# Rotary embedding over eight batches: row 0 of batch 0 is stored behind rows 1 to 15, and the first five batches are loaded without a store between

## The chip, the cores and the metric

The kernel runs on one core of one Trainium2 chip. The metric is the device time of one execution in microseconds (us). The kernel before took 316.6 us in the median of three runs (316.54 to 318.12).

## The reference

`x` is 8 x 2048 x 16 x 64 in f32 (batch, sequence, heads, head size), `cos` and `sin` are 2048 x 32. The first and second half of each head are rotated against one another:

```python
x1 = x[..., :head_dim // 2]
x2 = x[..., head_dim // 2:]
cos = cos[None, :, None, :]
sin = sin[None, :, None, :]
out1 = x1 * cos - x2 * sin
out2 = x1 * sin + x2 * cos
return np.concatenate([out1, out2], axis=-1).astype(np.float32)
```

## The kernel before, in words

**Tiling.** Of a batch's 2048 positions, partition p of 128 holds 16 neighbouring ones. These 16 are the "rows" in what follows (index j, `J` = 16): "row 0" of a batch is the first position of every partition, 128 x 1024 values, 512 KB in f32. A whole batch is 8 MB in f32. On the chip the work is in f16: `buf` (line 47) has five places of one batch each, and batch b has place b mod 5.

**Transfers.** All big transfers are issued by POOL (GpSimd) and change the type on the way: `load` (L62, issue on L71) reads f32 and writes f16 into `buf`; `store` (L73, issue on L81) reads f16 and writes f32 to the output. A call with n = 2 moves two batches in one transfer. `in_ring` (L51) ties each of them to the one before, so that POOL issues them in the order written; it makes POOL wait for nothing. The waits come from the data: a store waits for VectorE's last operation on its rows, a load for the landing of the stores that read its place of `buf`. POOL issues in order, so whatever is written behind a waiting store waits too. All of POOL's transfers are in queue q0. SP (SyncE) has q1: at the start it issues `sin` (L40), the first two rows of batch 0 into the f32 tile `head` (L41) and `cos` (L45), at the end one store of the last two rows of batch 7 (L135).

**Arithmetic.** ScalarE turns `sin`, `cos` and `head` into f16 (L104 to L110); `head` goes into rows 0 and 1 of batch 0's place (L106), so load 0 brings only rows 2 to 15. `rotate` (L83) does three VectorE operations on a batch in place: the halves swapped and multiplied by sin into `v` (L92), the batch multiplied by cos (L98), and the sum (L100). Batch 0 is rotated in two calls, rows 0 and 1 first (`JA` = 2), then rows 2 to 15.

**Order around the change.** It is written out by hand from L102 on. Loads 0 and 1 are issued; rows 0 and 1 are rotated (L111); row 0 is stored (L112); then come loads 2+3 in one transfer and load 4 (L113, L114); rows 2 to 15 of batch 0 are rotated (L115) and its rows 1 to 15 stored (L116); rotate 1 and store 1, rotate 2 and store 2 (L117 to L120); loads 5+6 and 7 (L121, L122), which take the places of batches 0, 1 and 2; then rotate 3 and 4 and store both, 5 and 6 and store both, and rotate 7, which leaves in three parts (L130, L131, L135).

Of the kernel before, what the change touches and what calls it, by code (L numbers as in the profile page):

```python
# [1 line left out]

# [4 lines left out]


@with_exitstack  # L10
def kernel(
    ctx: ExitStack,
    tc: tile.TileContext,
    x: bass.AP,
    cos: bass.AP,
    sin: bass.AP,
    out: bass.AP,
):
    nc = tc.nc
    f16 = mybir.dt.float16  # L20
    f32 = mybir.dt.float32

    B, S, H, D = x.shape
    Dh = D // 2
    P = nc.NUM_PARTITIONS
    J = S // P
    NBUF = 5

    const_pool = ctx.enter_context(tc.tile_pool(name="rope_const", bufs=1))
    io_pool = ctx.enter_context(tc.tile_pool(name="rope_io", bufs=1))  # L30
    tmp_pool = ctx.enter_context(tc.tile_pool(name="rope_tmp", bufs=1))

    JA = 2
    head = const_pool.tile([P, JA, H, D], f32)
    x0 = x[0].rearrange("(p j) h d -> p j (h d)", j=J)
    sin_f = const_pool.tile([P, J, Dh], f32)
    cos_f = const_pool.tile([P, J, Dh], f32)
    cos_h = const_pool.tile([P, J, Dh], f16)
    sin_h = const_pool.tile([P, J, D], f16)
    nc.sync.dma_start(out=sin_f, in_=sin.rearrange("(p j) d -> p j d", j=J))  # L40
    nc.sync.dma_start(  # L41
        out=head.rearrange("p j h d -> p (j h d)"),
        in_=x0[:, 0:JA, :].rearrange("p j f -> p (j f)"),
    )
    nc.sync.dma_start(out=cos_f, in_=cos.rearrange("(p j) d -> p j d", j=J))  # L45

    buf = io_pool.tile([P, NBUF, J, H, D], f16)

    ring = []

    def in_ring(dma):  # L51
        if ring:
            tc.add_manual_dep(
                dma.ins,
                ring[-1].ins.name,
                mybir.DependencyInfo(mybir.DependencyClass.NoSync, mybir.DependencyReason.DATA),
                reason="order of the ring",
            )
        ring.append(dma)
        return dma  # L60

    def load(b, n=1):  # L62
        k = b % NBUF
        if n == 1:
            j0 = JA if b == 0 else 0
            dst = buf[:, k, j0:J, :, :].rearrange("p j h d -> p (j h d)")
            src = x[b].rearrange("(p j) h d -> p j (h d)", j=J)[:, j0:J, :].rearrange("p j f -> p (j f)")
        else:
            dst = buf[:, k : k + n, :, :, :].rearrange("p b j h d -> p b (j h d)")
            src = x[b : b + n].rearrange("b (p j) h d -> p b (j h d)", j=J)  # L70
        in_ring(nc.gpsimd.dma_start(out=dst, in_=src))  # L71

    def store(b, n=1, j0=0, j1=J):  # L73
        k = b % NBUF
        if n == 1:
            src = buf[:, k, j0:j1, :, :].rearrange("p j h d -> p (j h d)")
            dst = out[b].rearrange("(p j) h d -> p j (h d)", j=J)[:, j0:j1, :].rearrange("p j f -> p (j f)")
        else:
            src = buf[:, k : k + n, :, :, :].rearrange("p b j h d -> p b (j h d)")
            dst = out[b : b + n].rearrange("b (p j) h d -> p b (j h d)", j=J)  # L80
        return in_ring(nc.gpsimd.dma_start(out=dst, in_=src))  # L81

    def rotate(b, j0=0, j1=J):  # L83
        v = tmp_pool.tile([P, J, H, D], f16)
        n = j1 - j0
        js = slice(j0, j1)
        xt = buf[:, b % NBUF, js, :, :]
        shape = [P, n, H, 2, Dh]
        sin_b = sin_h[:, js, :].rearrange("p j (e d) -> p j e d", e=2).unsqueeze(2).to_broadcast(shape)
        cos_b = cos_h[:, js, :].unsqueeze(2).to_broadcast([P, n, 2 * H, Dh])  # L90
        xe = xt.rearrange("p j h (e d) -> p j h e d", e=2)
        nc.vector.tensor_mul(  # L92
            out=v[:, js, :, :].rearrange("p j h (e d) -> p j h e d", e=2),
            in0=xe[:, :, :, ::-1, :],
            in1=sin_b,
        )
        xw = xt.rearrange("p j h (e d) -> p j (h e) d", d=Dh)
        nc.vector.tensor_mul(out=xw, in0=xw, in1=cos_b)  # L98
        xa = xt.rearrange("p j h d -> p (j h d)")
        nc.vector.tensor_add(out=xa, in0=xa, in1=v[:, js, :, :].rearrange("p j h d -> p (j h d)"))  # L100

    load(0)  # L102
    load(1)
    nc.scalar.copy(out=sin_h[:, :, Dh:D], in_=sin_f)  # L104
    nc.scalar.mul(out=sin_h[:, :, 0:Dh], in_=sin_f, mul=-1.0)  # L105
    nc.scalar.copy(  # L106
        out=buf[:, 0, 0:JA, :, :].rearrange("p j h d -> p (j h d)"),
        in_=head.rearrange("p j h d -> p (j h d)"),
    )
    nc.scalar.copy(out=cos_h, in_=cos_f)  # L110
    rotate(0, 0, JA)  # L111
    store(0, 1, 0, 1)  # L112
    load(2, 2)  # L113
    load(4)  # L114
    rotate(0, JA, J)  # L115
    store(0, 1, 1, J)  # L116
    rotate(1)  # L117
    store(1)
    rotate(2)
    store(2)  # L120
    load(5, 2)  # L121
    load(7)  # L122
    rotate(3)
    rotate(4)
    store(3, 2)
    rotate(5)
    rotate(6)
    store(5, 2)
    rotate(7)
    gate = store(7, 1, 0, 9)  # L130
    store(7, 1, 9, J - JA)  # L131
    last = buf[:, 7 % NBUF, J - JA : J, :, :].rearrange("p j h d -> p (j h d)")
    dst = out[B - 1].rearrange("(p j) h d -> p j (h d)", j=J)[:, J - JA : J, :].rearrange("p j f -> p (j f)")
    nc.scalar.copy(out=head.rearrange("p j h d -> p (j h d)"), in_=last)  # L134
    end = nc.sync.dma_start(out=dst, in_=head.rearrange("p j h d -> p (j h d)"))  # L135
    tc.add_manual_dep(
        end.ins,
        gate.ins.name,
        mybir.DependencyInfo(mybir.DependencyClass.Sync, mybir.DependencyReason.DATA),
        reason="the last rows go out behind this part",  # L140
    )


# [1 line left out]
_INS = ['x', 'cos', 'sin']  # L145
_OUTS = [((8, 2048, 16, 64), 'float32')]


# [23 lines left out]
```

## Time and profile before

| What | Value |
|---|---|
| Median of three runs | 316.6 us |
| The profiled execution's own time | 316.6 us |
| Its span | 314.8 us |
| VectorE (DVE) busy | 209.1 us, 66%, 27 operations |
| ScalarE (ACT) busy | 6.8 us |
| POOL busy | 8.6 us |
| One VectorE operation on a whole batch | 8.69 us |
| VectorE idle before L92, mostly for a load | 51.4 us |
| POOL idle before a store (L81), for VectorE's sum | 219.4 us |
| POOL idle before a load (L71), mostly for stores to land | 49.7 us |

The span runs from the first instruction of the profile to the last. "Busy" counts the engine's own operations; an instruction that issues a transfer is over long before its data has moved. Idle time of an engine is put down to what ended it. Of an issue the profile gives the size and the time until the transfer has landed; a load's size there is that of its f16 side, a store's that of its f32 side.

### The profile page before, as it was taken

To read this page: it belongs to the slowest core of one execution; us is meant where nothing else is said; L and a number is where in the kernel's file an instruction comes from. 1 tells how busy PE (TensorE), PEld (TensorE's weight loads), DVE (VectorE), ACT (ScalarE), POOL (GpSimd) and SP (SyncE) were. 2 spreads that over 40 slices of the span, in tenths; PEclk is the share of its full clock that TensorE was granted. 3 is DMA by queue.
4 is the path that set the end of the run, shared out by engine and by line. 5 is a ranking of instruction groups with operands and counts; after the bars stand their busy time and mean duration, and the time that the engine had idled before them with its cause. 6 is when DMAs were issued, how large, how long until landed. Compare 5 with 4: busy or idle time off the path is not lost.

```text
span 314.8 us, 115 instructions
## 1 busy us (share of the span) xinstructions
DVE 209.1 (66%) x27; ACT 6.8 (2%) x6; POOL 8.6 (3%) x18
## 2 busy tenths in 40 slices
DVE  0105999999499999999950000899999999910000
ACT  3200000000000000000000000000000000020000
POOL 1002000000000000000010000000000000010000
DMA  9899999999999899999999999999999999999998
GB/s 284 187 262 200 200 266 200 200 262 204 200 200 317 382 492 407 400 400 533 400 200 208 258 200 200 229 237 333 400 491 441 400 400 525 408 400 400 433 427 339
DMA packets 3104, 101.71 MB, mean 323 GB/s; under 512 B 288, under 2 KB 288, under 8 KB 672
## 3 DMA queue, kind: packets, MB, share of 16 engines
q0 software_dynamic: 2528, 99.09, 98.1%
q1 hardware_dynamic: 576, 2.62, 2.2%
HBM read 67.63 MB, written 67.11 MB: 428 GB/s over the span
## 4 chain that ended last, share of the span: by engine, by line
DVE 66%; another core or an unknown queue 13%; DMA 8%; ACT 1%; issue 0%; SPq 0%; DVEq 0%; ACTq 0%
DVE buf L98 22%; DVE buf L100 22%; DVE v L92 22%; DMA cos_f<-in_cos_dram 8%; ACT head L134 1%; ACT cos_h L110 0%; SPq L41 0%; SPq L40 0%; DVEq L92 0%; ACTq L134 0%
## 5 line engine op out<-in xcount | busy, mean ns | idle before, releaser
L92 DVE TENSOR_TENSOR v<-buf,sin_h 128x16384 f16<-128x16384 f16 (+2 forms) x9 | 69.7, 7744 | 51.4 <-DMA buf<-in_x_dram 41.2
L98 DVE TENSOR_TENSOR buf<-buf,cos_h 128x16384 f16<-128x16384 f16 (+2 forms) x9 | 69.7, 7744 | 15.8 <-ACT cos_h L110 15.5
L100 DVE TENSOR_TENSOR buf<-buf,v 128x16384 f16<-128x16384 f16 (+2 forms) x9 | 69.7, 7744 | 0.3
L81 POOL DMA_DIRECT2D out_dram<-buf x8 | 4.7, 586 | 219.4 <-DVE buf L100 219.4
L134 ACT CAST head<-buf 128x2048 f32<-128x2048 f16 x1 | 1.9, 1898 | 249.9 <-DVE buf L100 249.9
L71 POOL DMA_DIRECT2D buf<-in_x_dram x6 | 3.7, 628 | 49.7 <-DMA out_dram<-buf 48.9
L106 ACT CAST buf<-head 128x2048 f16<-128x2048 f32 x1 | 1.9, 1897 | 3.5 <-DMA head<-in_x_dram 3.5
L104 ACT ACT_TABLE_LOAD x1 | 1.3, 1283 | 0.7 <-PEq L156 0.7
L110 ACT CAST cos_h<-cos_f 128x512 f16<-128x512 f32 x1 | 0.6, 617 | 16.1 <-DMA cos_f<-in_cos_dram 16.1
L104 ACT CAST sin_h<-sin_f 128x512 f16<-128x512 f32 x1 | 0.6, 617 | 1.4 <-DMA sin_f<-in_sin_dram 1.4
L105 ACT ACTIVATE sin_h<-sin_f 128x512 f16<-128x512 f32 x1 | 0.6, 624 | 0.0
L156 POOL MEMSET const-float32-0.0<- 128x1 f32 x1 | 0.1, 100 | 0.2 <-issue 0.2
L156 POOL MEMSET const-bfloat16-1.0<- 128x1 bf16 x1 | 0.1, 103 | 0.0
L156 POOL MEMSET const-float32-1.0<- 128x1 f32 x1 | 0.1, 100 | 0.0
L156 POOL MEMSET const-uint8-127<- 128x1 uint8 x1 | 0.1, 100 | 0.0
## 6 DMA issues: line engine op xcount, KB each, us to landing
buf<-in_x_dram POOLq DMA_DIRECT2D x2, 8192.0 KB, 55.2
buf<-in_x_dram POOLq DMA_DIRECT2D x3, 4096.0 KB, 57.4
out_dram<-buf POOLq DMA_DIRECT2D x1, 7680.0 KB, 68.3
out_dram<-buf POOLq DMA_DIRECT2D x1, 4608.0 KB, 28.6
buf<-in_x_dram POOLq DMA_DIRECT2D x1, 3584.0 KB, 22.3
out_dram<-buf POOLq DMA_DIRECT2D x1, 2560.0 KB, 34.1
head<-in_x_dram SPq DMA_DIRECT2D x1, 1024.0 KB, 6.9
out_dram<-head SPq DMA_DIRECT2D x1, 1024.0 KB, 8.4
```

Of the source, the lines that this page charges most:

```text
L71: in_ring(nc.gpsimd.dma_start(out=dst, in_=src))
L81: return in_ring(nc.gpsimd.dma_start(out=dst, in_=src))
L92: nc.vector.tensor_mul(out=v[:, js, :, :].rearrange("p j h (e d) -> p j h e d", e=2), in0=xe[:, :, :, ::-1, :], in1=sin_b,)
L98: nc.vector.tensor_mul(out=xw, in0=xw, in1=cos_b)
L100: nc.vector.tensor_add(out=xa, in0=xa, in1=v[:, js, :, :].rearrange("p j h d -> p (j h d)"))
L104: nc.scalar.copy(out=sin_h[:, :, Dh:D], in_=sin_f)
L105: nc.scalar.mul(out=sin_h[:, :, 0:Dh], in_=sin_f, mul=-1.0)
L106: nc.scalar.copy(out=buf[:, 0, 0:JA, :, :].rearrange("p j h d -> p (j h d)"), in_=head.rearrange("p j h d -> p (j h d)"),)
L110: nc.scalar.copy(out=cos_h, in_=cos_f)
L134: nc.scalar.copy(out=head.rearrange("p j h d -> p (j h d)"), in_=last)
L156: nc = _bacc.Bacc("TRN2", target_bir_lowering=False, num_devices=1)
```

## The change

Row 0's store no longer stands ahead of loads 2+3 and 4, but behind the store of rows 1 to 15 and ahead of rotate 1. Loads 2+3 and 4 are issued right behind loads 0 and 1, ahead of ScalarE's first instruction in the text. The transfers themselves, their sizes and shapes stay, as do all operations of VectorE and ScalarE.

```diff
     load(0)
     load(1)
+    load(2, 2)
+    load(4)
     nc.scalar.copy(out=sin_h[:, :, Dh:D], in_=sin_f)
...
     nc.scalar.copy(out=cos_h, in_=cos_f)
     rotate(0, 0, JA)
-    store(0, 1, 0, 1)
-    load(2, 2)
-    load(4)
     rotate(0, JA, J)
     store(0, 1, 1, J)
+    store(0, 1, 0, 1)
     rotate(1)
     store(1)
```

## The prediction

> **What bounds the kernel now.** I read the page's slices and queue rows first, then the chain of waits, then the timeline of POOL (which issues all big transfers), then windows cut at the landings. The profiled execution took 316.6 us, span 314.8, so 1.8 us lie outside the span; 316.6 is also the median of the three runs.
>
> ```profile
> DMA  9899999999999899999999999999999999999998
> ...
> q0 software_dynamic: 2528, 99.09, 98.1%
> q1 hardware_dynamic: 576, 2.62, 2.2%
> HBM read 67.63 MB, written 67.11 MB: 428 GB/s over the span
> ```
>
> The 16 DMA engines are busy in every slice, and POOL's queue q0 has 98.1% of their time. 134.7 MB cross HBM. The chain of waits, in order of time, seems to say otherwise:
>
> ```profile
> 69.70 8.69 DVE buf L100
> 78.40 4.89 another core or an unknown queue
> ...
> 153.19 8.69 DVE buf L100
> 161.88 36.10 another core or an unknown queue
> ```
>
> It names VectorE for 66%, but twice breaks off at a transfer: VectorE starts again at 83.3 when the load of batches 2 and 3 has landed, and at 198.0 when that of batches 5 and 6 has. The second gap, 36.1 us, is the queue's doing. Who feeds the queue, and how early?
>
> ```profile
> 1.24 1.21 POOL L71 DMA_DIRECT2D buf<-in_x_dram  x2 [0.80 <-PEq L167]
> ...
> 29.53 0.54 POOL L81 DMA_DIRECT2D out_dram<-buf  x1 [27.08 <-DVE buf L100]
> 30.06 1.26 POOL L71 DMA_DIRECT2D buf<-in_x_dram  x2
> ...
> 52.52 0.54 POOL L81 DMA_DIRECT2D out_dram<-buf  x1 [21.19 <-DVE buf L100]
> ```
>
> POOL issues loads 0 and 1 at 1.24, then waits 27 us for VectorE's sum of the first two rows, issues row 0's store, and 0.5 us later the loads of 2, 3 and 4. These are late only for POOL. From issue to landing, the store and the first of the loads took:
>
> ```profile
> out_dram<-buf POOLq DMA_DIRECT2D x1, 512.0 KB, 15.2
> buf<-in_x_dram POOLq DMA_DIRECT2D x1, 8192.0 KB, 53.2
> ```
>
> Load 1 (issued about 1.85, landing 41.6 us later) lands at 43.5, row 0's store at 29.53 + 15.2 = 44.7, loads 2 and 3 at 30.06 + 53.2 = 83.3. So the store waits 14 us in the queue, and the loads behind it are handed over 14.6 us before the engines can begin them. The same is done for the rest: load 4 lands at 102.6, the stores of batch 0's other rows, 1 and 2 at 120.8, 140.1 and 159.4, loads 5+6 and 7 at 198.0 and 217.3, stores 3+4 and 5+6 at 256.0 and 294.6. In windows cut there (DMA share and GB/s are last; a load's GB/s count its f16 side, half of what it reads):
>
> ```profile
> 44.70:83.30 38.60, 33.59 (x4) 0.00 (x0) 1.08 (x2) 1.00 1.01 217
> 83.30:102.60 19.30, 19.15 (x3) 0.00 (x0) 0.00 (x0) 1.00 1.00 241
> 102.60:120.80 18.20, 18.13 (x3) 0.00 (x0) 0.53 (x1) 1.00 1.02 436
> 120.80:140.10 19.30, 19.23 (x3) 0.00 (x0) 0.00 (x0) 1.00 1.02 435
> ```
>
> The share is 1.0 throughout. One batch (8.39 MB of f32) takes 19.3 us in either direction, 435 GB/s: 38.6 / 2 for the loads, 19.3 for a store. The kernel is one full queue from the first packets to the last, and its time is the sum of the queue's parts.
>
> On this the Trainium skill (DMA: Bandwidth & Descriptors, "Where 436 GB/s comes from") says two things: the ports allow 435 GB/s, but for transfers between HBM and SBUF the HBM's share of about 358 GB/s binds. By the second, 134.7 MB would take 376 us, an estimate; the trace's 435 GB/s decides against it here.
>
> **The change, part by part.**
>
> *Row 0's store leaves the stretch between the loads.* The queue loses 44.7 - 43.5 = about 1.25 us there (0.524 MB at 435 GB/s would be 1.21). Loads 2+3 land at 82.0, load 4 at 101.3.
>
> *It comes back behind that of rows 1 to 15.* It needs the sum of rows 0 and 1 alone (VectorE done at 29.2), and POOL issues it right behind the other one, at about 53. The queue reaches them at 101.3: rows 1 to 15 land at 119.5 (18.2 later), row 0 at 120.8. From there on store 1 lands at 140.1 as before. What can its cost be in the new place? The trace has no small store between two big stores. In the records its 128 packets took 0.189 us each, eight per engine, 1.51 us; the landings say 1.25, since neighbours overlap. Upper end: nothing overlaps, +0.26. Lower end: it costs its bytes at full rate and a turn from load to store and back is saved, -0.05; more can't go, as its bytes remain. I take 0, by the near agreement of 1.25 with 1.21, and keep -0.05 to +0.26.
>
> *Loads 2, 3 and 4 are issued at about 2.5 to 3.7.* The row at 30.06 gives 1.26 us of POOL for both issues. Behind them on POOL is the store of rows 1 to 15, which waits for VectorE until 52.2, so this delays nobody. They wait for no buffer: five exist and these are first used here. What is queued per engine rises little: eight packets per batch make 8 + 8 + 16 + 8 = 40 at 3.7 us, against about 5 + 8 + 16 + 8 = 37 at 31.3 before. If POOL had to wait for room, it would have until 43.5 to hand over loads 2 and 3. The cost is 0 from these sides. Only the very start is not covered: a queue that starts empty (below).
>
> *VectorE.* Batch 2's first product starts at 82.0 in place of 83.3, and store 2 can be issued at 108.5 in place of 109.8. The queue wants it at 140.1: 31 us early instead of 30. Loads 5+6 wait on POOL for the landings of both stores of batch 0 and of store 1, at 140.1 as before, 19 us ahead of their turn at 159.4. Later orders keep their times: store 3+4 is issued at 162.2 and wanted at 217.3, store 5+6 at 250.7 and wanted at 256.0. That last cover, 5.3 us, is the thinnest, and both of its ends hang on the landing at 198.0, so it does not shrink. The last stores (276.9, wanted at 294.6) and SP's closing store follow.
>
> **Sum:** -1.25 + 1.25 + 0 = 0; span 314.8, time 316.6 us.
>
> **Rivals.**
>
> *The chain view is right* and the 1.25 us gained at 83.3 reaches the end: 315.3 (-0.4%). For it: the 4.89 us wait is on the chain. Against: the next one, 36.1 us, ends at a landing that the queue sets, and in a full queue row 0's bytes have only moved. Only a dry queue after 83.3 could keep the gain, and the windows show none.
>
> *Four issues in a row hold up the first load* (slower than before). Place: load 0 at the start.
>
> ```profile
> 3.00:5.00 2.00, 0.00 (x0) 1.15 (x2) 0.00 (x0) 1.00 0.98 415
> 5.00:8.00 3.00, 0.00 (x0) 0.00 (x0) 0.00 (x0) 1.00 1.53 346
> ```
>
> From 3 to 5 us the engines are at 0.98 with SP's head rows; load 0's first packet starts at 5.28 in the packet records, just as the head's last ones end (5.6), though POOL issued it at 1.24. Either it was ready and stood behind the head, or its descriptors came at 5.3 because load 1's were made first. In the second case two more issues hurt. Mild form: the 1.26 us of POOL are added, load 0 starts at 6.5, +1.26 at most, 317.9 (+0.4%); SP's cos packets would fill part. Strong form: 4.04 us for two issues (1.24 to 5.28) become 8.1 for four, load 0 starts at 9.3, some 4.0 late, of which cos (eight packets of about 0.1 us per engine) fills 0.8: +3.2, 319.8 (+1.0%). It decides from the point where the descriptors come later than 5.6, when the head is through. For it: no record shows any of load 0's packets among the head's. Against: POOL's rows show each issue as an instruction of its own, 0.6 us.
>
> By the Trainium skill (the same page, "Latency and other measured facts") POOL's path has its first byte after about 1 us, and (in "Queues, rings and completion order") an engine takes turns between its queues packet by packet. By both, load 0 would have mixed with the head from about 3 us, and the change would leave the start alone. After 7.3 us cos and load 0 do alternate in the records; before 5.28 load 0 is absent, so at least one of the two does not hold there. That is why this rival keeps a chance.
>
> *The rate changes* when 40 MB of loads run with no store between. Witness against: load batches before and after row 0's store, and 5 to 7 behind three whole stores, all take 19.3 (load 1 takes 19.9 with cos beside it). 0.5% of the time would need 2% on the 78 us of loads 1 to 4; the rows differ by 0.3%. Prices: 318.2 or 315.0.
>
> *The change does not do what it says*: POOL issues loads 2 to 4 later than 3.7 for some reason. Up to 43.5 that gives 316.6 too, so it stands with the forecast.
>
> **How the numbers follow.** A measurement here tells about 0.5% (1.6 us) from no change. Forecast (316.6, with the late issue): 0.78, same. Mild start delay (up to 317.9): 0.08, same. Strong start delay (319.8): 0.06, slower. Chain view (315.3): 0.03, same. Rate: 0.05, slower 0.03, faster 0.02. So faster 0.02, same 0.89, slower 0.09. Range: below, 316.6 - 0.05 - 0.6 for the scatter of runs (the three shown differ by up to 1.6, though two by 0.06) gives 315.9. Above, 316.6 + 0.26 + 1.26 gives 318.1. Outside lie the strong delay, the chain view and the rate, 0.14.
>
> **What would show it.** Right: loads 2+3 landing at 82.0 and VectorE's first product of batch 2 there; POOL issuing four loads by 3.8; rows 1 to 15 landing at 119.5, row 0 at 120.8, store 1 at 140.1; VectorE's wait before batch 5 ending at 198.0 and now 37.4 us long; DMA slices all 9 (or 8). Wrong: a DMA gap at 5 to 9 us and everything after it shifted alike (start rival); a landing at 198.0 that comes 1.25 early with the end (chain view); 19.3 us per batch no longer the step between landings (rate).

## The result, and the profile after

The changed kernel takes 317.33 us in the median (317.14 to 318.07), the kernel before 316.62 in the runs beside it: a ratio of 1.0022, with a 95% interval of 1.0016 to 1.0029. That is 0.7 us, less than the 0.5% that the prediction called a change, but clear of the scatter: the kernel became slower where no difference was forecast. The profiled execution took 317.37 us, its span 315.6 (before: 316.6 and 314.8). The ratios in this document leave out runs that lie over 1.5% above the fastest of their kernel (one each in e2, e7, f5 and f6); the medians include them.

The page's queue rows are as good as unchanged; the queue is still full throughout:

```profile
DMA  9899999999999899999999999999999999999998
...
q0 software_dynamic: 2528, 99.09, 98.2%
...
HBM read 67.63 MB, written 67.11 MB: 427 GB/s over the span
```

The timeline of POOL shows that the change does what it says: four loads in one go, over by 3.71, and both stores of batch 0 together:

```profile
1.24 2.47 POOL L71 DMA_DIRECT2D buf<-in_x_dram  x4 [0.80 <-PEq L167]
...
52.57 1.07 POOL L81 DMA_DIRECT2D out_dram<-buf  x2 [48.85 <-DVE buf L100]
```

The DMA issues give the landings (the last number of a row is the time from issue to landing). Loads 2+3, issued at about 2.4, land at 81.6, load 4 at 102.1, rows 1 to 15 at 120.35, row 0 at 121.6:

```profile
buf<-in_x_dram POOLq DMA_DIRECT2D x1, 8192.0 KB, 79.2
buf<-in_x_dram POOLq DMA_DIRECT2D x1, 4096.0 KB, 99.0
...
out_dram<-buf POOLq DMA_DIRECT2D x1, 7680.0 KB, 67.8
out_dram<-buf POOLq DMA_DIRECT2D x1, 512.0 KB, 68.5
```

In the chain of waits the first gap has shrunk from 4.89 to 3.17 us, and the second has grown from 36.10 to 38.52, more than the first gave:

```profile
78.45 3.17 another core or an unknown queue
...
160.21 38.52 another core or an unknown queue
```

Windows cut at the landings show in which transfer the time went (columns: window, its length, busy time of VectorE, ScalarE and POOL, TensorE's clock, DMA share, GB/s; a packet is booked where it starts, so the shares of neighbours can differ a little):

```profile
23.60:43.00 19.40, 16.09 (x4) 0.62 (x1) 0.00 (x0) 1.00 1.00 216
43.00:81.60 38.60, 35.31 (x5) 0.00 (x0) 1.60 (x3) 1.00 1.01 217
81.60:102.10 20.50, 20.32 (x3) 0.00 (x0) 0.00 (x0) 1.00 1.00 227
102.10:120.35 18.25, 18.18 (x3) 0.00 (x0) 0.53 (x1) 1.00 0.93 393
...
121.60:140.90 19.30, 19.23 (x3) 0.00 (x0) 0.00 (x0) 1.00 1.02 435
...
160.20:198.70 38.50, 0.01 (x1) 0.00 (x0) 1.27 (x2) 1.00 1.01 218
198.70:218.10 19.40, 19.21 (x3) 0.00 (x0) 0.00 (x0) 1.00 1.00 243
```

Load 4 takes 20.5 us where every other load of a whole batch in these windows takes 19.3 or 19.4. Its DMA share is 1.00: the engines do not idle, their packets are longer. Load 1 has become faster, 19.4 us; this is its window in the kernel before, 19.9 us long:

```profile
23.60:43.50 19.90, 16.64 (x4) 0.62 (x1) 1.79 (x3) 1.00 0.92 199
```

The trace's records of single packets say which ones. A load packet (64 KB read, 32 KB written, eight per batch and engine) takes 2.43 us. Two sets of 16 packets, one per engine, differ. In each kernel the long ones are the last load packets ahead of the queue's first store (mean us, in brackets the excess):

| | load 1's last packets, at 40 us | load 4's last packets, at 98 us | first store behind |
|---|---|---|---|
| before | 2.83 (+0.39) | 2.43 (0) | row 0, at 42.7 us |
| after | 2.43 (0) | 3.66 (+1.23) | rows 1 to 15, at 101.5 us |

So the sum is -0.4 at load 1 and +1.2 at load 4, while row 0's store costs nearly the same in both places (1.26 between landings before, 1.22 after). That is +0.75 or so, all of it ahead of 103 us. From there on both traces run in step, 0.7 to 0.8 us apart (store 1 lands at 140.1 and 140.9, loads 5+6 at 198.0 and 198.7). Ends of loads behind which a store follows later (load 7, at about 217) show nothing in either kernel. It is the queue's **first turn from loads to a store** that costs, once in an execution, and the price differs.

### The profile page after: what moved, and what is told of

It is laid out like the page before. It is cut to its first block, busy times and chain, and to the rows that moved or that the text cites. A ratio compares the mean times of both kernels' runs of the same rounds, so it can differ in the third digit from the quotient of the medians.

```text
span 315.6 us, 114 instructions
## 1 busy us (share of the span) xinstructions
DVE 209.1 (66%) x27; ACT 6.8 (2%) x6; POOL 8.6 (3%) x18
## 4 chain that ended last, share of the span: by engine, by line
DVE 66%; another core or an unknown queue 13%; DMA 8%; ACT 1%; issue 0%; SPq 0%; DVEq 0%; ACTq 0%
DVE buf L98 22%; DVE buf L100 22%; DVE v L92 22%; DMA cos_f<-in_cos_dram 8%; ACT head L134 1%; ACT cos_h L112 0%; SPq L41 0%; SPq L40 0%; DVEq L92 0%; ACTq L134 0%
## 5 line engine op out<-in xcount | busy, mean ns | idle before, releaser
L98 DVE TENSOR_TENSOR buf<-buf,cos_h 128x16384 f16<-128x16384 f16 (+2 forms) x9 | 69.7, 7744 | 15.7 <-ACT cos_h L112 15.5
```

## The experiments

In what follows, "the wait" is the mean time by which those 16 packets exceed 2.43 us. All edits are against the changed kernel, if nothing else is said. The expectations call such a delay "late packets", a "lump" (all of it in one place) or, later, a "debt". The first theory was that the size of the first store's packets sets the price; its main rival was that the price grows with the loads that ran before it.

### Which store stands first: e1_small_first, e11_small_first_again, e8_two_rows_first, f2_whole_batch

```diff
     rotate(0, JA, J)
-    store(0, 1, 1, J)
     store(0, 1, 0, 1)
+    store(0, 1, 1, J)
```

> As the changed kernel, but row 0's store goes ahead of that of rows 1 to 15; both still follow all five loads. Theory (first store): the last load packet in front of the queue's first store is late on every engine, once in an execution, and the more so the bigger that store's packets are: 0.4 us with 4 KB packets (before, at 40 us), 1.2 us with 60 KB packets (after, at 98 us). It expects 2.83 us for those packets at 98 us, 0.4 over the 2.43 of the others, and 316.6 us. Rival (long run): the price comes from the run of 40 MB of loads, whatever store follows. It expects 3.65 us for these packets and 317.3 us. Rival (end of the first burst of issues): the last packet issued before POOL's first wait is late; no size in it, so again 3.65 and 317.3.

Measured: 317.43 us, ratio 1.0024 (1.0014 to 1.0035). The wait at 98 us was only 0.09, but in this profile load packets between 50 and 85 us were up to 0.11 late each, 0.9 us together. The time speaks for the rival, the wait for the theory; one profile could not settle it.

> The run with row 0's store ahead of the big one behind five loads, once more. There the lump at 98 us was 0.1 us, but load packets from 50 to 85 us were 0.1 us late each, 1.0 us in all. Theory (a debt that is paid in any case): again 1.0 to 1.2 us in all, in a lump at 98 us or spread; if a lump, the spread was one way among others in which the same comes out. Rival (two causes that met by chance): 0.1 to 0.6 us in all.

Measured: 317.16 us in one run, a wait of 0.76 at 98 us and 0.06 at 81. So here the wait comes in one place again, as in the changed kernel, and row 0 being first does not make it cheap there. Why the first profile had it spread out stays open.

```diff
-    store(0, 1, 1, J)
-    store(0, 1, 0, 1)
+    store(0, 1, 0, 2)
+    store(0, 1, 2, J)
```

> As the changed kernel, but behind the five loads the first store is that of rows 0 and 1 (8 KB packets) and the second that of rows 2 to 15. Theory (the first run of loads): 1.2 us in all before the first store, as one lump at 98 us or spread over the loads, as in the run with row 0 first; 317.35. Rival (size): about 0.5 us, 316.7.

Measured: a wait of 1.03, 317.38 us, ratio 1.0028 (1.0017 to 1.0039). The theory of the packets' size expected about 0.5, so packet size as such is out.

```diff
-    store(0, 1, 1, J)
-    store(0, 1, 0, 1)
+    store(0)
```

> As the changed kernel, but batch 0 leaves in one store (64 KB packets) behind the five loads. Row 0's own store is gone: 1.22 us of the queue less, 19.3 - 18.2 = 1.1 more. Both theories: 1.2 us late at 98 us, 317.2.

Measured: a wait of 1.08, 317.37 us, ratio 1.0020 (1.0008 to 1.0032). Without row 0's own transfer the wait stays and the time hardly moves: the split itself costs nothing to speak of.

### When the loads are issued: e2_pause_only

```diff
     load(0)
     load(1)
-    load(2, 2)
-    load(4)
...
     rotate(0, 0, JA)
+    pause = const_pool.tile([P, 16], f16)
+    nc.gpsimd.tensor_copy(out=pause, in_=buf[:, 0, 0, 0, 0:16])
+    load(2, 2)
+    load(4)
```

> As the changed kernel, but POOL waits at the place of before: a copy of 128 x 16 values on POOL reads the sum of rows 0 and 1, and loads 2+3 and 4 are issued behind it at about 30 us; no store stands there. Theory (first store): nothing late at 40 us, 3.65 us for load 4's last packets at 98 us, 317.3 us. Rival (end of the first burst of issues): the late packets are load 1's last, at 40 us, and load 4's are 2.43. Rival (long run): as the theory, it does not tell these two apart.

Measured: nothing at 40 us, a wait of 1.34 at 98, 317.41 us, ratio 1.0024 (1.0015 to 1.0033). In the timeline of POOL the loads go out at 36.85, since the tiny copy lasts as long as VectorE's operation beside it:

```profile
29.26 7.65 POOL L113 COPY pause<-buf 128x16 f16<-128x16 f16 x1 [26.81 <-DVE buf L100]
36.85 1.26 POOL L71 DMA_DIRECT2D buf<-in_x_dram  x2
52.48 1.06 POOL L81 DMA_DIRECT2D out_dram<-buf  x2 [14.37 <-DVE buf L100]
```

and load 4's window is as in the changed kernel:

```profile
81.60:102.20 20.60, 20.46 (x3) 0.00 (x0) 0.00 (x0) 1.00 1.00 226
```

Of the two things that the change did, the early issue is therefore innocent; the missing store is the cause.

### How many loads run before the first store: e3_big_early, e6_row_after_2, e7_big_after_2, e12_row_after_0

```diff
     load(2, 2)
-    load(4)
...
     store(0, 1, 0, 1)
+    load(4)
```

> As the changed kernel, but load 4 goes behind the two stores of batch 0, so that the big store (60 KB packets) comes first and after 32 MB of loads in place of 40. Theory (first store): the last packets of loads 2+3, at about 78 us, take 3.65 us, load 4's take 2.43, 317.3 us. Rival (long run): the price falls with the run, to some 3.4 us and 317.1, if it grows evenly from 0.4 at 16 MB to 1.2 at 40 MB. Rival (end of the first burst): late packets at 78 us too; not told apart here.

Measured: a wait of 0.73 at 79 us, load 4 undisturbed, 317.60 us, ratio 1.0030 (1.0019 to 1.0040). Less than either theory expected.

For e6 load 2 goes alone, and row 0's store, then loads 3 and 4, follow the first rotation; for e7 the same with both stores behind all of batch 0's rotation.

```diff
     load(0)
     load(1)
-    load(2, 2)
-    load(4)
+    load(2)
...
     rotate(0, 0, JA)
+    store(0, 1, 0, 1)
+    load(3)
+    load(4)
     rotate(0, JA, J)
     store(0, 1, 1, J)
-    store(0, 1, 0, 1)
```

> As before, but row 0's store (4 KB packets) stands behind load 2 in place of load 1, so the run of loads ahead of it is 24 MB; loads 3 and 4 follow it as transfers of their own. Theory (the first run of loads): 0.55 us on load 2's last packets at about 60 us, between the 0.4 at 16 MB and the 0.7 at 32, then nothing; 316.75. Rival (size): 0.4 us, 316.6.

> As the changed kernel, but both stores of batch 0, the big one (60 KB packets) first, stand behind load 2, so the run ahead is 24 MB; loads 3 and 4 follow them. Theory (the first run of loads): 0.55 us at about 60 us, 316.7. Rival (size): 1.2 us there, 317.3.

Measured: row 0 behind load 2 waits 0.62, 316.91 us, ratio 1.0014 (1.0003 to 1.0025); the big store there waits 1.25, 317.72 us, ratio 1.0034 (1.0024 to 1.0044). At one place, 60 us, the two stores pay different prices, and the big one pays at 60 what it pays at 98: the run of loads does not set the price. The profiles of e3, e6 and e7 show another difference as well. SP's head came late (7.6, 15.7 and 9.8 us to landing, 6.9 before; it took 8.9 to 9.3 in several other runs too), and to the end of POOL's queue the first and the last of the 16 engines stayed 0.8 (e3, e6) and 1.5 us (e7) apart, where it is 0.3 to 0.7 in most other runs. The times of these three are therefore no clean price of the wait.

e12 is the kernel before with this edit:

```diff
     nc.sync.dma_start(out=sin_f, in_=sin.rearrange("(p j) d -> p j d", j=J))
+    nc.sync.dma_start(out=cos_f, in_=cos.rearrange("(p j) d -> p j d", j=J))
     nc.sync.dma_start(
         out=head.rearrange("p j h d -> p (j h d)"),
         in_=x0[:, 0:JA, :].rearrange("p j f -> p (j f)"),
     )
-    nc.sync.dma_start(out=cos_f, in_=cos.rearrange("(p j) d -> p j d", j=J))
...
     load(0)
-    load(1)
...
+    nc.scalar.copy(out=cos_h, in_=cos_f)
     nc.scalar.copy(
         out=buf[:, 0, 0:JA, :, :].rearrange("p j h d -> p (j h d)"),
         in_=head.rearrange("p j h d -> p (j h d)"),
     )
-    nc.scalar.copy(out=cos_h, in_=cos_f)
     rotate(0, 0, JA)
     store(0, 1, 0, 1)
+    load(1)
     load(2, 2)
```

> As before, but SP loads cos ahead of head, ScalarE turns it into f16 ahead of head's rows, and row 0's store stands behind load 0, so that the run of loads ahead of the first store is 8 MB. Theory (the first run of loads, 0.025 us per MB): 0.2 us late on load 0's last packets at 21 us in place of 0.4 at 40, 316.4 us. Rival (size of the first store's packets): 0.4 us still, 316.6.

Measured: 325.87 us, ratio 1.0317 (1.0292 to 1.0343); the profile is of an execution of 328.63. The edit did not make the case that it was meant to make, so neither theory is tested by its time. Behind cos, head's 1 MB alternated with load 0 packet by packet and took 24.7 us to land, so the first rotation ended after load 0, and the queue ran dry:

```profile
26.10:28.00 1.90, 0.00 (x0) 1.67 (x1) 0.00 (x0) 1.00 0.00 0
28.00:30.00 2.00, 1.71 (x2) 0.22 (x1) 0.00 (x0) 1.00 0.00 0
30.00:32.00 2.00, 1.97 (x2) 0.00 (x0) 0.00 (x0) 1.00 0.00 0
32.00:33.40 1.40, 1.37 (x1) 0.00 (x0) 1.09 (x3) 1.00 0.00 0
```

It tells one thing: row 0's store, on idle engines and with load 1 only just issued behind it, did not settle the matter. Load 4's last packets waited 0.83 all the same, and load 1's first ones were 0.59 late.

### Smaller early stores: e4_sp_first, e10_sp_row, e5_tiny_early, e9_quarter_row, f1_half_row

SP's early store, behind cos in q1 (for e10 the whole row, `[:, J - JA, :]`, in place of one head; the closing store, which writes the same bytes, is made to wait for it):

```diff
+    tail = out[B - 1].rearrange("(p j) h d -> p j (h d)", j=J)[:, J - JA, 0:D]
+    early = nc.sync.dma_start(out=tail, in_=head[:, 0, 0, :])
```

> As the changed kernel, and SP also stores 128 x 64 values of head (256 B packets, 32 KB) early, into a part of the output that the closing store overwrites; it stands in q1 behind cos. If what is paid once is the engines' first write to the output, from whichever queue: load 4's last packets take 2.43 us, and with under 0.4 us paid at about 25 to 40 us the time is 316.2 to 316.7. If it is the first store of POOL's queue: load 4's last packets take 3.65 us still, 317.4 us with the added bytes. The rival of the long run expects the latter as well.

> As the run with SP's early store, but a whole row of head (128 x 1024 values, 4 KB packets, 512 KB, as much as row 0's store moves), so 1.2 us of extra work for the DMA engines; its packets alternate with load 1 and following. If any store of enough bytes settles it: nothing late at 98 us, and 317.33 + 1.2 - 1.2 + 0.4 = some 317.7. If it must be POOL's queue, or a store that stands between the loads in one queue: 1.2 us at 98 us, some 318.6.

Measured: waits of 1.15 and 0.92 at 98 us; 317.50 us, ratio 1.0028 (1.0019 to 1.0038), and 318.57, ratio 1.0067 (1.0054 to 1.0080). A first write to the output from another queue does not settle it, even as large as row 0.

POOL's early store of a part of row 0, between loads 1 and 2:

```diff
     load(0)
     load(1)
-    load(2, 2)
-    load(4)
...
     rotate(0, 0, JA)
+    tiny = out[0].rearrange("(p j) h d -> p j (h d)", j=J)[:, 0, 0:D]
+    in_ring(nc.gpsimd.dma_start(out=tiny, in_=buf[:, 0, 0, 0, :]))
+    load(2, 2)
+    load(4)
```

> As the run with POOL's pause and no early store, but in place of the pause POOL stores the first head of row 0 alone (128 x 64 values, 256 B packets, 32 KB) between loads 1 and 2; the store of row 0 writes these bytes once more later. Theory (the first run of loads): a delay gathers over the loads ahead of the queue's first store, 0.4 us at 16 MB, 0.7 at 32, 1.2 at 40, and is paid when a store of any size ends the run; loads behind it pay nothing. It expects 0.4 us at 40 us, nothing at 98 us, 316.7 us. Rival (size of the first store's packets): under 0.4 us at 40 us and nothing at 98, 316.3 to 316.6. Rival (a tiny store ends nothing): 1.2 us at 98 us as without it, 317.4.

> As the run with the first head of row 0 stored early, but four heads of it (1 KB packets, 128 KB). So far the delay of the last load packets ahead of a store is 0 with 256 B and 0.4 us with 4 KB at 40 us, 0.6 with 4 KB at 60, 1.0 with 8 KB at 98, 1.2 with 60 KB; and after the 4 KB store none comes at 98, after the 256 B store 1.2 comes. Theory (a debt of the first run of loads that a store works off as far as it lasts): about 0.1 us at 40 us and 1.0 at 98; about 317.5 with the extra bytes (0.3 us). Rival (a store of some size ends the matter altogether): 0.1 at 40 and nothing at 98, 316.7.

Measured: with one head nothing at 40 us and 1.16 at 98, 317.43 us, ratio 1.0034 (1.0018 to 1.0050). With four heads (for e9) nothing to speak of at 40 and 0.95 at 98, 317.43 us, ratio 1.0031 (1.0019 to 1.0043).

f1 is the kernel before with its first two stores cut elsewhere (`piece(f0, f1)` stores these elements of each partition's 16 rows):

```diff
-    store(0, 1, 0, 1)
+    piece(0, 512)
...
-    store(0, 1, 1, J)
+    piece(512, J * H * D)
```

> As before, but the first store is half of row 0 (2 KB packets, 256 KB) and the second takes the rest of batch 0 in one piece (62 KB packets). The same bytes as before in the same number of transfers. Theory (the queued store's bytes): at the first turn from loads to a store in the full queue, the last load packets are late by the time of reading what stands next in the queue, up to some 32 KB of f16 per engine: 0.4 to 0.6 us with 16 KB (4 KB packets), 0.7 to 1.3 with 32 KB or more. It expects 0.2 us at 40 us. If that settles the later turn, 316.4 us and the fastest so far; if it doesn't, as with 256 B and 1 KB packets, about 1.0 us at 98 us and 317.4. Rival (a debt of the first run of loads): 0.4 at 40 us or the rest of it at 98, 316.6 or above.

Measured: 0.12 at 40 us and 0.59 at 98. 316.67 us, ratio 0.9998 (0.9987 to 1.0009): no better than before, and between the two cases of the expectation (316.4 and 317.4). But this run completes a row: the wait left at 98 us falls with the early store, 1.23, 1.16, 0.95, 0.59 and 0 us for 0, 1, 4, 8 and 16 KB of f16 per engine. The early store shortens the later wait according to its size; it does not simply end it.

### What in the early transfer counts: f4_inside_row, f3_f32_row, f5_f32_row_again, f6_inside_f16

Each puts one transfer of one row between loads 1 and 2, as e5 does, and keeps the later stores. f4 moves buf's row 0 (f16) into head (f32) on the chip; f3 and f5 store head's row (f32) to the output as it came, behind e2's pause, and the later store of row 0 overwrites it; f6 moves buf's row 0 into load 4's place, f16 to f16.

```diff
+    aside = head[:, 0, :, :].rearrange("p h d -> p (h d)")    # f6: buf[:, 4, 0, :, :]
+    in_ring(nc.gpsimd.dma_start(out=aside, in_=buf[:, 0, 0, :, :].rearrange("p h d -> p (h d)")))
```

> As the run with POOL's early tiny store, but in its place POOL moves row 0 of buf (f16) to head's first row (f32), inside the chip: 4 KB packets, 512 KB, nothing written to HBM. The later stores stay. Up to 1.2 us of extra work. Theory (the queued bytes that are read from the chip): 0.4 to 0.6 us at 40 us and none at 98, 316.1 + 1.2 + 0.5 = 317.8. Rival (it takes a write to HBM): nothing at 40 us, 1.2 us at 98, 318.5.

Measured: 0.40 at 40 us, nothing at 98, 317.91 us, ratio 1.0047 (1.0030 to 1.0065). The early transfer writes nothing to HBM, and it does what row 0's store did. The windows after it, loads 2+3 and load 4, both undisturbed:

```profile
44.60:83.20 38.60, 35.90 (x5) 0.00 (x0) 1.60 (x3) 1.00 1.01 217
83.20:102.50 19.30, 19.13 (x3) 0.00 (x0) 0.00 (x0) 1.00 1.00 241
```

> As the run with POOL's pause, and behind the pause POOL stores a row of head as it was loaded, f32 to f32 (4 KB packets, 512 KB, 32 KB per engine on the SBUF side), to row 0 of the output, which the later store of row 0 overwrites. 1.2 us of extra work. Without any lump the changed kernel would take 317.33 - 1.2 = 316.1. Theory (the queued store's bytes, counted where they are read): 32 KB, so about 1.0 us at 40 us, none at 98: 316.1 + 1.2 + 1.0 = 318.3. Rival (bytes counted where they are written, or the packets' size): 0.4 us at 40 us as with row 0 in f16, 317.7. If it has to do with the change of type: nothing at 40 us, 1.2 at 98, 318.5.

Measured: 318.55 us, ratio 1.0066 (1.0043 to 1.0090), but the profiled execution took 321.14, with one engine about 2 us behind. Its waits, 0.43 at 40 us and 1.27 at 98, are not used below, although they say the opposite of the repeat about the later turn:

> The run with the f32 row of head stored early, once more: in its profile one DMA engine had fallen 2 us behind the others. Theory (the lead of the reading side): before a store is written, the engine's reading must be some 1.2 us ahead of its writing; loads from the start have no such lead, so the first store waits for it, and once there it stays. A small f16 to f32 store builds it cheaply, since 16 KB per engine are read in 0.6 us while 32 KB are written in 1.2. f32 to f32 reads and writes at one pace, so the only gain is the wait itself: 0.4 us at 40 us, 0.8 at 98, 316.1 + 1.2 + 1.2 = 318.5. Rival (any 16 KB read from the chip in POOL's queue settle it): 0.4 at 40, nothing at 98, 317.7.

Measured: 318.51 us, ratio 1.0060 (1.0046 to 1.0074), and a clean profile: 0.98 at 40 us, nothing at 98. The theory had the total nearly right (1.2 expected) and the split wrong: all of it was paid at the first turn. The window of load 1 and that of load 4:

```profile
23.70:44.10 20.40, 17.30 (x4) 0.62 (x1) 9.39 (x4) 1.00 0.93 196
...
83.90:103.20 19.30, 19.13 (x3) 0.00 (x0) 0.00 (x0) 1.00 1.00 241
```

> As the run that moves row 0 inside the chip early, but without a change of type, f16 to f16 (2 KB packets, 256 KB, 16 KB read per engine as with row 0's store), into the place that load 4 fills later. 0.6 us of extra work. Theory (the lead of the reading side): one pace for reading and writing, so the lead gained is only the wait, 0.1 to 0.4 us at 40 us; the rest of 1.2, 0.8 to 1.1, comes at 98; 316.1 + 0.6 + 1.2 = 317.9. Rival (any 16 KB read from the chip in POOL's queue settle it): 0.1 to 0.4 at 40, nothing at 98, 316.8 to 317.1.

Measured: 0.22 at 40 us and 0.73 at 98, 317.93 us, ratio 1.0038 (1.0024 to 1.0052). The theory expected both waits. The same 16 KB are read per engine as in f4 and before, but the later turn is not freed; load 4 is late again:

```profile
82.50:102.40 19.90, 19.77 (x3) 0.00 (x0) 0.00 (x0) 1.00 1.01 234
```

So the bytes read are not it. That the change of type decides does not follow, for f6 also writes only half as much as f4, 16 KB per engine and not 32. f1 wrote 16 KB too, with the change of type, and left 0.59 to f6's 0.73; this is load 4's window in f1:

```profile
82.40:102.20 19.80, 19.64 (x3) 0.00 (x0) 0.00 (x0) 1.00 1.01 237
```

And f5 wrote 32 KB without a change of type and left nothing. In the profiles used here the later wait goes with the bytes that the early transfer writes.

### What adds up

Take an engine's pace in this trace, 435 / 16 = 27 GB/s, for reading and for writing alike; that both sides go at this pace is an assumption. Then 16 KB take 0.60 us. A transfer from f16 to f32 would be read in half the time in which it is written, and its reading would get ahead of its writing by that half. The table adds this gain to the two waits, and, beside it, the time of writing to the later wait alone:

| early transfer, per engine | wait at 40 us | gained by reading | wait at 98 us | sum of the three | time of writing | wait at 98 us and writing |
|---|---|---|---|---|---|---|
| none (after, e2) | 0 | 0 | 1.23, 1.34 | 1.2 to 1.3 | 0 | 1.2 to 1.3 |
| 1 KB f16 to f32 (e5) | 0 | 0.04 | 1.16 | 1.20 | 0.08 | 1.24 |
| 4 KB f16 to f32 (e9) | 0 | 0.15 | 0.95 | 1.10 | 0.30 | 1.25 |
| 8 KB f16 to f32 (f1) | 0.12 | 0.30 | 0.59 | 1.01 | 0.60 | 1.19 |
| 16 KB f16 to f32 (before) | 0.39 | 0.60 | 0 | 0.99 | 1.20 | 1.20 |
| the same, on the chip (f4) | 0.40 | 0.60 | 0 | 1.00 | 1.20 | 1.20 |
| 16 KB f16 to f16 (f6) | 0.22 | 0 | 0.73 | 0.95 | 0.60 | 1.33 |
| 32 KB f32 to f32 (f5) | 0.98 | 0 | 0 | 0.98 | 1.20 | 1.20 |

The sum of the three is 0.95 to 1.34 us in every row, about 1.0 to 1.3, whatever its parts. Row 0 behind load 2 (e6) gives 0.62 + 0.60 = 1.22, the big store there (e7) 1.25. With nothing ahead, e8 and f2 paid 1.03 and 1.08, e11 and e3 only 0.82 and 0.73, so single profiles scatter by some tenths. One theory that fits is that of a lead: by the time the stores run, each engine's reading is about 1.0 to 1.2 us ahead of its writing; the loads from the start bring no such lead; the first store waits until there is one; once there, it stays, so later turns are free. By it, row 0's store between the loads got 0.6 us of the lead for nothing, while its own writing kept the engine busy and load 2 was already being read.

A second account fits the waits at 98 us at least as well: the early transfer shortens the later wait by the time that it takes to write, whatever its type. The last column is 1.19 to 1.34 in every row (where 32 KB are written it says little, since no wait can be less than nothing). This account does not give the wait at 40 us, and there the type does matter: 0.39 and 0.40 against 0.98 when 32 KB are written, 0.12 against 0.22 when 16 KB are. No run tells the two accounts apart.

The Trainium skill (DMA: Bandwidth & Descriptors, "Two DMAs through the same engine are not ordered") says that descriptors start in order but are pipelined, and that an engine's read and write sides are separate queues. That is what such a lead would need; the page gives neither its size nor a price, and no run here shows reading apart from writing.

Shown are the waits and their places, that the issue time plays no part, and that a transfer in POOL's own queue between the loads shortens the later wait, the more the larger it is, to HBM or on the chip. Neither the lead nor the part of the type change in the later wait is shown. Still open: why the wait was spread out in e1, why the big store paid 0.73 in e3 and 1.25 in e7, why f3's profile left 1.27 where f5's left nothing, and why row 0's store on idle engines (e12) freed only part. That load 1's reading was not there yet to run ahead would explain the last; it was not tried.

## Why the prediction was right or wrong

- **The bound was right.** The queue is full, a batch takes 19.3 us in either direction, and VectorE's earlier start (81.7, forecast 82.0) is worth nothing. The chain-view rival is out: its 1.7 us at the first gap came back as 2.4 at the second.
- **The moved store's own price was right.** It is 1.22 us behind the big store, against 1.26 ahead of load 2, so -0.04; the range given was -0.05 to +0.26.
- **The early issue was right at nothing.** Four issues are over by 3.71, load 0's first packet again at 5.28, no gap; e2 shows it from the other side. The start rival is out in both forms, and so is the late issue. The rate rival is out as well: between the turns packets follow one another every 2.41 us in both traces.
- **The step that failed** is the price of the turn: "Lower end: it costs its bytes at full rate and a turn from load to store and back is saved, -0.05". The sum, -1.25 + 1.25 + 0, has no other term for a turn and so takes it to cost the same wherever the first store stands. It costs 0.39 before and 1.23 after, not 0.05 and not the same; +0.84 is what the sum lacked. Taking 0.05 from the landings of load 1 and row 0 (43.5 and 44.7) was the error: the wait lies ahead of the first of these two. A row of the prediction showed it, "load 1 takes 19.9 with cos beside it": in the changed kernel, with the same cos beside it, load 1 takes 19.4. And row 0's store was treated as bytes that could stand anywhere, though the trace before had one turn with a wait (load 1) and another without (load 4), and nothing said that the second owed its freedom to the first.
- **The numbers.** The forecast was 316.6, measured are 317.33, inside the range. Loads 2+3 landed at 81.6, 0.4 ahead of the forecast 82.0, as load 1's wait was gone; from load 4 on every landing came 0.7 to 0.9 late (102.1 for 101.3, 140.9 for 140.1, 198.7 for 198.0). That the change stayed under 0.5% came true, but by luck: no case of the prediction held the 0.7 us that happened, and the room above in its range was for the store's overlap and a late start, neither of which occurred.

## What to carry to other kernels

In a kernel that is one full DMA queue, a transfer is not only its bytes: look in the packet records at the last packets ahead of each change from loads to stores, compare the first change with the later ones, and count a wait there as part of the turn, not of the load. A landing-to-landing step hides a wait that lies ahead of the first landing. If the first store comes late, a part of it put early between the loads can pay for most of that first turn. Here 16 KB of f16 per engine, written as f32, brought the waits from 1.23 to 0.39 in all, and 8 KB to 0.71. An extra transfer made only for this does not pay: f4 freed the later turn and took 317.91 us, against 317.33 without it. And on a queue that had run dry (e12) the early store freed only part.

## What the runs showed of the hardware that was not expected

- The first turn from loads to stores in POOL's queue cost 0.7 to 1.3 us once in an execution; with an f16 to f32 transfer of 16 KB read per engine between the loads, the waits came to 0.4 in all. A copy on the chip (f4) did as well as a store to HBM.
- A POOL copy of 128 x 16 values beside VectorE's f16 operation took 7.65 us, as long as that operation (7.62).
- Head's 1 MB in SP's queue lands 6.9 us after its issue when only sin is ahead of it, and 24.7 when load 0's packets alternate with its own (e12): one 8 KB packet per 56 KB packet of the other queue.
